# State-space mixer: the second half's outputs in other PSUM tiles, products within a chunk first, the chunk table's products in one run

## The chip, the cores and the metric

The kernel runs on one core of a Trainium2 chip. The metric is the time of one execution on the device, in microseconds (us). The core's engines run side by side, each through its own queue in order: TensorE (PE: matmuls, with weight loads as PEld), VectorE (DVE), ScalarE (ACT), GpSimd (POOL) and SyncE (SP), which here issues nearly all DMAs. Matmuls write to PSUM, whose contents VectorE and ScalarE read.

## What is computed

Two decoder layers over 512 tokens of width 1024. Each runs three token mixers on the same input projection: A (RWKV-7), B (retention) and C, a diagonal complex state-space mixer (S5) in 32 groups of 16 channels and 64 states. Only C is touched:

```python
bu_re = jnp.einsum('gpc,bsgc->bsgp', bb_re, uf)
bu_im = jnp.einsum('gpc,bsgc->bsgp', bb_im, uf)
...
_, _, x_re, x_im = lax.associative_scan(combine, (a_re, a_im, bu_re, bu_im), axis=1)
y = (jnp.einsum('gcp,bsgp->bsgc', c_re.astype(f32), x_re)
     - jnp.einsum('gcp,bsgp->bsgc', c_im.astype(f32), x_im)
     + d_skip.astype(f32) * uf)
y = jax.nn.gelu(y.reshape(bsz, seq, C_WIDTH))
y = y * jax.nn.sigmoid(y @ w_glu.astype(f32) + b_glu.astype(f32))
```

## The kernel before

Mixer C cuts the 512 tokens into 64 chunks of 8. A scan over chunks gives the state ahead of each chunk; the output of a chunk is then a product with that state (a *lag product*, L490) plus a product with the chunk's own inputs through a table (a *product within a chunk*, L495). The groups are worked in two halves (`hf`) of 8 pairs.

`s5_prep` makes the tables. `ca` (powers times C), in four quarters on VectorE and POOL; `ba` (powers times B), turned by PE transposes (L402) and copied by ScalarE (L403); and the table `tt` (s5tt) for the products within a chunk. For `tt`, PE multiplies `bd` by `ca` for four m, two parts and four column strips (L411, one PSUM tile p); ScalarE copies the result to `s1gs` (L414), VectorE adds the skip term (L416), SP writes it to DRAM as gsc (L419) and reads it back in eight transfers, each into 16 partitions of s5tt (L423).

`s5_main` does for each half: 64 input products on PE (L460: `bre` in a PSUM tile m, `bim` in a tile p, 32 in each half of the groups); on VectorE four products that read them (L464 to L467), two scans (L471, L472) and the states `cx` (L479 to L484, after POOL's memsets of their first columns); then on PE into two PSUM tiles b the lag products (L490, 32 in the code, 64 instructions) and the products within a chunk (L495, 16 in the code, 32 instructions). Each of the two results goes through a GELU of two ScalarE and three VectorE steps (L500 to L504), and out to DRAM (yst, L506). Behind both halves four tiles yg are read back (L512) and split by ScalarE and VectorE (L179, L180 in `split`), and `s5_glu` multiplies them.

PSUM has four kinds of tiles, g, m, p and b, two of each. `cx` and the GELU's tile cg exist once, so their next use waits for the last one's end.

Around mixer C, PE works through blocks of the input projection (`proj_steps`): each loads a weight block (raw, L148), splits it (wh by ScalarE at L151, wl by VectorE at L155) and runs 24 matmuls (L169 to L171) into a tile g, which ScalarE evacuates (L609 and L610 for mixer A, L1078 for the gates). A scheduler with its own timeline of the program sets each engine's order from priorities when the program is built; on the chip each engine then keeps to that order and waits on semaphores. The blocks around `s5_main` are called g_1538, g_1572, g_1606 and g_1640 in layer 0 and g_10521 to g_10623 in layer 1, after their PSUM tiles. With two tiles g, g_1640 takes the room of g_1572 and can start when that is evacuated.

Of the kernel before, what the change touches and what calls it, by code (L numbers as in the profile page):

```python
# [80 lines left out]
class Hybrid:  # L81
# [224 lines left out]
    def s5_prep(self, pool, keep):  # L306
# [3 lines left out]
        nc, par = self.nc, self.par  # L310
        V, G, S, PE = nc.vector, nc.gpsimd, nc.scalar, nc.tensor
# [93 lines left out]
        gs = t("gs", (128, 4, 256))  # L405
        G.memset(gs[:, :, 0:128], 0.0)
        ps = self.pps().rearrange("p (m x) -> p m x", m=4)
        for m in range(4):
            for part in range(2):
                for j in range(4):  # L410
                    PE.matmul(ps[32 * j:32 * j + 32, m, :], lhsT=bd[part][:, 4 * m + j].rearrange("p g c -> p (g c)"),  # L411
                              rhs=self.ca[part][:, 4 * m + j, 0:8, :].rearrange("p k c -> p (k c)"), start=part == 0,
                              stop=part == 1, tile_position=(0, 32 * j))
        S.copy(out=gs[:, :, 128:256], in_=ps)  # L414
        for m in range(4):
            V.scalar_tensor_tensor(gs[:, m, 128:144], self.K[:, K_E16:K_E16 + 16], par[:, P_CD + m:P_CD + m + 1],  # L416
# [28 lines left out]
    def s5_main(self, pool, keep):  # L445
        nc, par = self.nc, self.par
        V, G, S, PE = nc.vector, nc.gpsimd, nc.scalar, nc.tensor
        page = lambda tag, bufs=1, dt=F32: pool.tile([128, T], dt, tag=tag, bufs=bufs, name=self.nm(tag))
        n8 = lambda t: t.rearrange("p (r n) -> p r n", n=64)
        H = (slice(0, 64), slice(64, 128))  # L450
        yst = self.dram.tile([4, 128, T], F32, name=self.nm("yst"))
        out = yst.rearrange("m (r g c) (t n) -> t c g (m r) n", g=2, c=16, t=8)
        for hf in range(2):
            prs = slice(8 * hf, 8 * hf + 8)
            bre, bim = self.mps(), self.pps()
            for part, b in ((0, bre), (1, bim)):
                for i in range(8):
                    for g in range(2):
                        pr = 8 * hf + i
                        PE.matmul(b[H[g], 64 * i:64 * i + 64], lhsT=self.ba[:, part, pr, 64 * g:64 * g + 64],  # L460
                                  rhs=self.uc[:, 2 * pr + g, :], start=True, stop=True)
            c, s, dec = (x[:, prs].rearrange("p r n -> p (r n)") for x in (self.rc, self.rs, self.dec))
            t1, t2, t3, t4 = page("c1"), page("c2"), page("c3"), page("c4")
            V.tensor_tensor(t1, bre, c, op=MUL)  # L464
            V.tensor_tensor(t4, bre, s, op=MUL)
            V.tensor_tensor(t2, bim, s, op=MUL)
            V.tensor_tensor(t3, bim, c, op=MUL)  # L467
            V.tensor_tensor(t1, t1, t2, op=ADD)
            V.tensor_tensor(t3, t3, t4, op=SUB)
            zr, zi = page("c2"), page("c4")  # L470
            V.tensor_tensor_scan(zr, dec, t1, 0.0, op0=MUL, op1=ADD)  # L471
            V.tensor_tensor_scan(zi, dec, t3, 0.0, op0=MUL, op1=ADD)  # L472

            x = [page("cx%d" % i).rearrange("p (r n) -> p r n", n=64) for i in range(2)]
            t5, t6 = page("c1"), page("c3")
            for v in x:
                G.memset(v[:, :, 0:1], 0.0)
            d = lambda v: n8(v)[:, :, 0:63]
            V.tensor_tensor(x[0][:, :, 1:], d(zr), d(c), op=MUL)  # L479
            V.tensor_tensor(d(t5), d(zi), d(s), op=MUL)  # L480
            V.tensor_tensor(x[1][:, :, 1:], d(zr), d(s), op=MUL)
            V.tensor_tensor(d(t6), d(zi), d(c), op=MUL)
            V.tensor_tensor(x[0][:, :, 1:], x[0][:, :, 1:], d(t5), op=SUB)
            V.tensor_tensor(x[1][:, :, 1:], x[1][:, :, 1:], d(t6), op=ADD)  # L484
            yp = [self.bps(), self.bps()]
            for i in range(8):
                for part in range(2):
                    for g in range(2):
                        ca = self.ca[part][H[g], 8 * hf + i, 1:9, :].rearrange("p k c -> p (k c)")
                        PE.matmul(yp[g][:, 64 * i:64 * i + 64], lhsT=ca, rhs=x[part][H[g], i, :],  # L490
                                  start=i == 0 and part == 0, stop=False, skip_group_check=True)
            for g in range(2):
                for i in range(8):
                    gr = 2 * (8 * hf + i) + g
                    PE.matmul(yp[g][:, 64 * i:64 * i + 64], lhsT=self.tt[:, gr, :], rhs=self.uc[:, gr, :],  # L495
                              start=False, stop=True, skip_group_check=True)
            for g in range(2):

                ps, y, g1 = yp[g], page("cy", 2), page("cg1")
                S.activation(g1, ps, AF.Square)  # L500
                V.tensor_scalar(g1, g1, 0.044715, 1.0, op0=MUL, op1=ADD)
                V.tensor_tensor(g1, g1, ps, op=MUL)
                S.activation(g1, g1, AF.Tanh, scale=math.sqrt(2.0 / math.pi))
                V.scalar_tensor_tensor(y, g1, 1.0, ps, op0=ADD, op1=MUL)  # L504
                for t in range(8):
                    nc.sync.dma_start(out=out[t, :, g, prs], in_=n8(y)[16 * t:16 * t + 16])  # L506
        self.yg = []
        yhl = keep.tile([128, 2, 4, T], F32R, tag="s5ba", name=self.nm("cyhl"))
        yh, yl = ([yhl[:, i, m, :] for m in range(4)] for i in range(2))
        for m in range(4):  # L510
            y = page("cyg", 4)
            nc.sync.dma_start(out=y, in_=yst[m])  # L512
            self.split(yh[m], yl[m], y, 0.5)
            self.yg.append(y)
        self.yghl = yh, yl
# [823 lines left out]
```

## Time and profile before

| | |
|---|---|
| time, median of 3 runs | 2138.72 us (2137.79 to 2141.57) |
| the profiled execution, its time | 2140.92 us |
| its span, first to last instruction | 2138.8 us |
| mean granted TensorE clock | 0.983 of full speed |
| PE busy | 2081.7 us, 97% |
| VectorE / ScalarE / POOL busy | 57% / 35% / 7% |
| PE's wait for L504 ahead of L490 | 4.6 us in 4 waits |

The page counts busy time on each engine. The lists of waits say which instruction an engine waited for, the timeline lists instructions in order of time, and the rows by stretches give busy time, the granted TensorE clock (1.00 is 2.4 GHz, 0.50 is 1.2 GHz) and what the DMA engines moved. Mixer C's main part lies at 116 to 168 us in layer 0 and at 1178 to 1231 us in layer 1. A wait of an engine that is not on the path to the end costs nothing; here PE is on it nearly all the time.

### The profile page before, as it was taken

The numbers are of one execution on the slowest core, as the hardware profiler recorded it, in microseconds if no ns is written. First come the engines' busy times: TensorE is split into PE (matmuls) and PEld (weight loads), VectorE is DVE, ScalarE is ACT, GpSimd is POOL, SyncE is SP. The second block draws the span as 40 slices with busy tenths as digits, with TensorE's granted clock in tenths as the row PEclk, the third lists the DMA queues.
The fourth block names the chain that finished last, engine by engine and source line by source line (L and its number), as shares of the span: only waits on it lengthen the run. The fifth ranks groups of instructions, "written<-read, shape, count | busy, mean of one in ns | idle before, by whom it ended". The sixth has DMA issues, their size and how long they took to land.

```text
span 2138.8 us, 31693 instructions
## 1 busy us (share of the span) xinstructions
PE 2081.7 (97%) x12784; PEld 1717.1 (80%) x12784; DVE 1220.4 (57%) x2048; ACT 744.0 (35%) x1079; POOL 145.3 (7%) x302
## 2 busy tenths in 40 slices
PE   8999999999999999999999999999999999999998
PEld 7788887787787888888887887787787878888886
DVE  7764467675656734343596534676756666343345
ACT  4423344343332323133254234433333324132231
POOL 1300022021000000000013000220220000000000
PEclk9999999999999999999999899999999999999999
DMA  9584642233655323223274856332335453233331
GB/s 220 149 139 144 192 120 73 88 86 80 197 155 196 100 88 118 73 97 110 96 183 132 120 174 177 99 95 74 93 108 185 148 168 119 80 108 89 99 114 53
DMA packets 365170, 263.95 MB, mean 123 GB/s; under 512 B 79328, under 2 KB 309856, under 8 KB 364896
## 3 DMA queue, kind: packets, MB, share of 16 engines
q1 hardware_dynamic: 365024, 261.93, 43.7%
q8 instruction: 100, 1.64, 0.3%
q14 instruction: 46, 0.38, 0.1%
HBM read 218.89 MB, written 42.99 MB: 122 GB/s over the span
## 4 chain that ended last, share of the span: by engine, by line
PE 85%; DVE 8%; DMA 3%; issue 2%; ACT 2%; SPq 0%; DVEq 0%; ACTq 0%
PE g L169 24%; PE g L170 24%; PE g L171 23%; DVE wl L155 2%; PE b L1038 1%; PE m L731 1%; PE p L899 1%; PE b L1018 1%; ACT wh L151 1%; PE p L883 1%; PE p L872 1%; PE b L171 1%; PE b L170 1%; DMA raw<-in_w_out 1%; PE b L169 1%
## 5 line engine op out<-in xcount | busy, mean ns | idle before, releaser
L151 ACT CAST wh<-raw 128x1024 fp32r<-128x1024 f32 x312 | 326.4, 1051 | 788.3 <-PE g L170 387.4
L169 PE MATMUL g<-xh,wh 128*128 128x512 f32 (+1 forms) x1472 | 579.2, 394 | 8.2 <-DVE bg L1000 3.3
L155 DVE TENSOR_TENSOR wl<-raw,wh 128x1024 fp32r<-128x1024 f32 x312 | 382.9, 1232 | 345.5 <-ACT wh L151 339.2
L170 PE MATMUL g<-xl,wh 128*128 128x512 f32 (+1 forms) x1472 | 566.3, 385 | 0.2
L171 PE MATMUL g<-xh,wl 128*128 128x512 f32 (+1 forms) x1472 | 565.4, 384 | 0.0
L169 PEld LDWEIGHTS g<-xh,wh 128*128 128x128 f32 x1472 | 279.4, 190 | 69.2 <-issue 7.0
L171 PEld LDWEIGHTS g<-xh,wl 128*128 128x128 f32 x1472 | 279.4, 190 | 55.5 <-issue 1.2
L170 PEld LDWEIGHTS g<-xl,wh 128*128 128x128 f32 x1472 | 280.0, 190 | 54.2 <-issue 3.5
L170 PE MATMUL g<-wl,hh 128*128 128x512 f32 x512 | 201.2, 394 | 1.4 <-DVE wl L155 1.4
L171 PE MATMUL g<-wh,hl 128*128 128x512 f32 x512 | 201.1, 393 | 0.0
L169 PE MATMUL g<-wh,hh 128*128 128x512 f32 x512 | 200.2, 392 | 0.0
L170 PEld LDWEIGHTS g<-wl,hh 128*128 128x128 f32 x512 | 96.3, 188 | 24.3 <-DVE wl L155 2.2
L169 PEld LDWEIGHTS g<-wh,hh 128*128 128x128 f32 x512 | 96.2, 188 | 22.0
L171 PEld LDWEIGHTS g<-wh,hl 128*128 128x128 f32 x512 | 96.1, 188 | 21.3
L169 PE MATMUL g<-yh,wh 128*128 128x512 f32 x256 | 104.1, 407 | 0.0
L1281 DVE TENSOR_TENSOR yb<-yb,g 128x512 f32<-128x512 f32 x48 | 32.9, 686 | 121.9 <-PE g L171 121.9
L171 PE MATMUL g<-yh,wl 128*128 128x512 f32 x256 | 100.0, 391 | 0.0
L170 PE MATMUL g<-yl,wh 128*128 128x512 f32 x256 | 99.8, 390 | 0.0
L791 POOL TENSOR_TENSOR TLt<-NL,TL 128x120 f32<-128x120 f32 (+14 forms) x120 | 49.1, 409 | 643.5 <-DMA NL<-nsc 634.7
L169 PE MATMUL g<-wh,xh 128*128 128x256 f32 x256 | 77.1, 301 | 0.4 <-DVE bsw L971 0.3
L170 PE MATMUL g<-wl,xh 128*128 128x256 f32 x256 | 72.4, 283 | 0.0
L171 PE MATMUL g<-wh,xl 128*128 128x256 f32 x256 | 72.2, 282 | 0.0
(346 smaller groups left out, 2746.6 us busy)
## 6 DMA issues: line engine op xcount, KB each, us to landing
raw<-in_w_in SPq DMA_DIRECT2D x132, 512.0 KB, 4.1
raw<-in_w_ff SPq DMA_DIRECT2D x128, 512.0 KB, 4.1
raw<-in_w_branch SPq DMA_DIRECT2D x32, 512.0 KB, 4.3
gs<-gth SPq DMA_DIRECT2D x48, 256.0 KB, 2.3
gth<-gs SPq DMA_DIRECT2D x48, 256.0 KB, 3.1
raw<-in_w_out SPq DMA_DIRECT2D x16, 512.0 KB, 5.4
zs<-az SPq DMA_DIRECT2D x24, 256.0 KB, 4.2
s5tt<-gsc SPq DMA_DIRECT2D x16, 256.0 KB, 12.0
```

The lines of the kernel that those rows point to most:

```text
L151: nc.scalar.copy(out=wh, in_=raw)
L155: eng.tensor_tensor(wl, raw, wh.bitcast(F32), op=SUB)
L169: mm(out, lhsT=wh, rhs=xh, start=first, stop=False)
L170: mm(out, lhsT=wh, rhs=xl, start=False, stop=False)
L171: mm(out, lhsT=wl, rhs=xh, start=False, stop=last)
L731: PE.matmul(ps[h][:, i, :].rearrange("p (s i) -> p s i", i=64), lhsT=BK[H[h], c, :], rhs=rhs, start=True, stop=True)
L791: G.tensor_tensor(tmp[:, :, 0:n], NL[:, s:s + 1, s + 1:16].to_broadcast([128, 8, n]), TL[:, :, s:s + 1].to_broadcast([128, 8, n]), op=MUL)
L872: PE.matmul(ps[H[h], i, :].rearrange("p (s i) -> p s i", i=64), lhsT=Pt[H[h], 4 * g + i, :], rhs=AVX[H[h], h:3:2 - h, 4 * g + i, :], start ...
L883: PE.matmul(ps[H[h], i, :], lhsT=WM[H[h], 4 * g + i, :], rhs=AB[H[h], h, 4 * g + i, :], start=True, stop=True)
L899: PE.matmul(ps[:, h, :], lhsT=AB[:, h, c, :], rhs=AVX[:, h, c, :], start=h == 0, stop=c == 0, skip_group_check=True)
L1018: PE.matmul(ps[:, 0:n], lhsT=k[:, 128 * jc:128 * jc + 128], rhs=q[:, 128 * jc:T], start=True, stop=True)
L1281: V.tensor_tensor(y[t][:, s], y[t][:, s], ps, op=ADD)
```

## The change

The second half's two outputs are put into a tile m and a tile p, whose earlier contents are the first half's inputs `bre` and `bim`; the first half keeps tiles b. The products within a chunk are written ahead of the lag products and open the accumulation. In `s5_prep` the products for the table are chained in one order by `after` (an order on PE without a semaphore), the m with the last quarter of `ca` first.

```diff
--- before.py
+++ after.py
@@ -405,12 +405,18 @@
         gs = t("gs", (128, 4, 256))
         G.memset(gs[:, :, 0:128], 0.0)
         ps = self.pps().rearrange("p (m x) -> p m x", m=4)
-        for m in range(4):
+
+        last = None
+        for m in (3, 0, 1, 2):
             for part in range(2):
                 for j in range(4):
                     PE.matmul(ps[32 * j:32 * j + 32, m, :], lhsT=bd[part][:, 4 * m + j].rearrange("p g c -> p (g c)"),
                               rhs=self.ca[part][:, 4 * m + j, 0:8, :].rearrange("p k c -> p (k c)"), start=part == 0,
                               stop=part == 1, tile_position=(0, 32 * j))
+                    ins = nc.cur_bb.bb.instructions[-1]
+                    if last is not None:
+                        self.after(ins, last)
+                    last = ins
         S.copy(out=gs[:, :, 128:256], in_=ps)
         for m in range(4):
             V.scalar_tensor_tensor(gs[:, m, 128:144], self.K[:, K_E16:K_E16 + 16], par[:, P_CD + m:P_CD + m + 1],
@@ -482,18 +488,19 @@
             V.tensor_tensor(d(t6), d(zi), d(c), op=MUL)
             V.tensor_tensor(x[0][:, :, 1:], x[0][:, :, 1:], d(t5), op=SUB)
             V.tensor_tensor(x[1][:, :, 1:], x[1][:, :, 1:], d(t6), op=ADD)
-            yp = [self.bps(), self.bps()]
+
+            yp = [self.bps(), self.bps()] if hf == 0 else [self.mps(), self.pps()]
+            for g in range(2):
+                for i in range(8):
+                    gr = 2 * (8 * hf + i) + g
+                    PE.matmul(yp[g][:, 64 * i:64 * i + 64], lhsT=self.tt[:, gr, :], rhs=self.uc[:, gr, :],
+                              start=i == 0, stop=False, skip_group_check=True)
             for i in range(8):
                 for part in range(2):
                     for g in range(2):
                         ca = self.ca[part][H[g], 8 * hf + i, 1:9, :].rearrange("p k c -> p (k c)")
                         PE.matmul(yp[g][:, 64 * i:64 * i + 64], lhsT=ca, rhs=x[part][H[g], i, :],
-                                  start=i == 0 and part == 0, stop=False, skip_group_check=True)
-            for g in range(2):
-                for i in range(8):
-                    gr = 2 * (8 * hf + i) + g
-                    PE.matmul(yp[g][:, 64 * i:64 * i + 64], lhsT=self.tt[:, gr, :], rhs=self.uc[:, gr, :],
-                              start=False, stop=True, skip_group_check=True)
+                                  start=False, stop=part == 1, skip_group_check=True)
             for g in range(2):
 
                 ps, y, g1 = yp[g], page("cy", 2), page("cg1")
```

The chunk table's products on PE in layer 0, before: L411 is the group of four matmuls of one m and one part, p_638 its PSUM tile, g_1085 and g_1122 are projection blocks of mixer A, m_600 and m_619 (L402) transposes for `ba`. The last of the eight groups, early in g_1122; the one before it stands eight matmuls ahead:

```order
L171 MATMUL g_1085<-xh_84,wl_1083 128x512
L169 MATMUL g_1122<-xh_84,wh_1118 128x512
L411 MATMUL p_638<-s5ca_73_514,s1bd_71_506 32x128 x4
L170 MATMUL g_1122<-xl_85,wh_1118 128x512
L171 MATMUL g_1122<-xh_84,wl_1120 128x512
```

The same place of the change (L413 is L411's new line), in block g_1159, the next one:

```order
L413 MATMUL p_638<-s5ca_73_514,s1bd_71_506 32x128 x4
L413 MATMUL p_638<-s5ca_72_513,s1bd_70_505 32x128 x4
L413 MATMUL p_638<-s5ca_73_514,s1bd_71_506 32x128
L402 MATMUL m_619<-ident,s1bp_614 128x128 x4
L413 MATMUL p_638<-s5ca_73_514,s1bd_71_506 32x128 x3
L413 MATMUL p_638<-s5ca_72_513,s1bd_70_505 32x128 x4
L171 MATMUL g_1159<-xh_84,wl_1157 128x512
```

Before, the eight groups lie one by one among the blocks g_900 to g_1122. Now one lies near the end of g_1122, and the other seven (28 matmuls) in one run after the fifth matmul of g_1159, with one group of transposes inside; 19 matmuls of g_1159 and the 24 of g_1196 stand between the run and the input products. In layer 1 the run lies after the 17th matmul of g_10105.

The input products on PE in layer 0 before (m_1232, p_1233 for the first half, m_1372, p_1373 for the second), with what follows; xh and xl are the split input:

```order
L460 MATMUL m_1232<-uc_376,s5ba_515 64x64 x15
L460 MATMUL p_1233<-uc_376,s5ba_515 64x64 x16
L460 MATMUL m_1372<-uc_376,s5ba_515 64x64 x16
L460 MATMUL p_1373<-uc_376,s5ba_515 64x64 x16
L169 MATMUL g_1538<-xh_84,wh_1534 128x512
```

And of the change (L460 is L466 now, L495 is L496, L490 is L502), with what each waits for:

```order
L466 MATMUL m_1372<-uc_376,s5ba_515 64x64 x13
L496 MATMUL b_1292<-uc_376,s5tt_678 128x64 [waits DMAHW5_49,DMAHW4_49,DMAHW6_49,DMAHW3_49,DMAHW7_49,DMAHW2_49,DMAHW1_49]
L496 MATMUL b_1292<-uc_376,s5tt_678 128x64 x7
L496 MATMUL b_1293<-uc_376,s5tt_678 128x64 x8
L466 MATMUL m_1372<-uc_376,s5ba_515 64x64 x2
L466 MATMUL p_1373<-uc_376,s5ba_515 64x64 x16
L496 MATMUL m_1432<-uc_376,s5tt_678 128x64 [waits DVE_49,PE_49]
L496 MATMUL m_1432<-uc_376,s5tt_678 128x64 x7
L496 MATMUL p_1433<-uc_376,s5tt_678 128x64 [waits DVE_49,PE_49]
```

Before, the input products are followed by blocks g_1538 and g_1572 (48 matmuls), the first half's L490 and L495, 19 matmuls of g_1606, the second half's L490 and L495, and the last five of g_1606. Now the first half's products within a chunk stand inside the input products, behind the DMAs of s5tt, and the second half's right behind them; then come 15 matmuls of g_1538, the first half's lag products, 9 and 11 of g_1538 and g_1572, the second half's lag products, 13 of g_1572, the 24 of g_1606, and g_1640. In layer 1 L496 stands behind all 32 input products of the first half and ahead of the second half's.

ScalarE in layer 0 before: L500 and L503 are the GELU's square and tanh, L179 the splits of yg, L151 and L1078 the cast and the evacuation for the blocks:

```order
L151 CAST wh_1670<-raw_1668 128x1024
L1078 ACTIVATE gth_1597<-g_1572,hbg_1529 128x512
L500 ACTIVATE cg_222_1343<-b_1292 128x512
L503 ACTIVATE cg_222_1343<-cg_222_1343 128x512
L500 ACTIVATE cg_224_1358<-b_1293 128x512
L503 ACTIVATE cg_224_1358<-cg_224_1358 128x512
L179 ACTIVATE cyhl_1512<-cyg_1513 128x512
L179 ACTIVATE cyhl_1512<-cyg_1517 128x512
```

And of the change (L507 and L510 are the square and the tanh now, L1085 the evacuation):

```order
L151 CAST wh_1636<-raw_1634 128x1024
L1085 ACTIVATE gth_1563<-g_1538,hbg_1529 128x512
L507 ACTIVATE cg_224_1358<-b_1293 128x512
L510 ACTIVATE cg_224_1358<-cg_224_1358 128x512
L507 ACTIVATE cg_240_1483<-m_1432 128x512
L179 ACTIVATE cyhl_1512<-cyg_1513 128x512
L179 ACTIVATE cyhl_1512<-cyg_1517 128x512
L510 ACTIVATE cg_240_1483<-cg_240_1483 128x512
L507 ACTIVATE cg_242_1498<-p_1433 128x512
L510 ACTIVATE cg_242_1498<-cg_242_1498 128x512
L151 CAST wh_1670<-raw_1668 128x1024
L1085 ACTIVATE gth_1597<-g_1572,hbg_1529 128x512
```

The cast wh_1670 and the evacuation of g_1572 have moved from ahead of the GELUs to behind the two splits and the second half's first GELU. In layer 1 these two stand ahead of the last tanh instead of behind it.

On VectorE the second half's last state products still stand ahead of the first half's GELU. On SP, gsc and the eight reads of s5tt move behind one more weight block and one more store of mixer A; one store of a gate and one weight block stand among the stores of yst.

## Rows read from the trace of the kernel before

**Rows 1.** The page, busy time, share of the span and instructions.
```profile
PE 2081.7 (97%) x12784; PEld 1717.1 (80%) x12784; DVE 1220.4 (57%) x2048; ACT 744.0 (35%) x1079; POOL 145.3 (7%) x302
```

**Rows 2.** Waits of PE: total us, times, longest us.
```profile
PE b L490 <- DVE cy L504: 4.6, 4, 2.3
```

**Rows 3.** Timeline of PE, layer 0, second half: start us, us, what [idle before].
```profile
152.57 6.49 PE L490 MATMUL b<-cx,s5ca 64*128 64x64 f32 x54 [2.03 <-DVE cy L504]
158.99 7.09 PE L495 MATMUL b<-uc,s5tt 128*128 128x64 f32 x32
165.84 0.77 PE L170 MATMUL g<-xl,wh 128*128 128x512 f32 x1
...
168.12 0.63 PE L169 MATMUL g<-xh,wh 128*128 128x512 f32 x1
```

**Rows 4.** Timeline of PE, layer 0, first half.
```profile
137.16 3.79 PE L490 MATMUL b<-cx,s5ca 64*128 64x64 f32 x64
140.87 3.79 PE L495 MATMUL b<-uc,s5tt 128*128 128x64 f32 x32
```

**Rows 5.** PE by stretches: us, busy us (count), granted clock, DMA share, GB/s.
```profile
152.50:159.00 6.50, 6.43 (x55) 0.55 0.34 56
...
165.80:170.20 4.40, 4.40 (x12) 0.50 0.28 47
170.20:175.00 4.80, 4.80 (x22) 0.99 0.79 217
```

**Rows 6.** Timeline of PE, layer 1, the first matmul of g_10623.
```profile
1230.80 0.63 PE L169 MATMUL g<-xh,wh 128*128 128x512 f32 x1
```

**Rows 7.** Timeline of PE, layer 0, around one group of L411.
```profile
101.31 0.40 PE L170 MATMUL g<-xl,wh 128*128 128x512 f32 x1
...
102.34 0.40 PE L169 MATMUL g<-xh,wh 128*128 128x512 f32 x1
```

**Rows 8.** Input products: PE by the stretch (layer 0), their first timeline row (layer 1).
```profile
122.17:126.05 3.88, 3.88 (x128) 1.00 1.23 185
...
1184.31 1.09 PE L460 MATMUL m<-uc,s5ba 128*64 128x64 f32 x29
```

**Rows 9.** Timeline of ScalarE, the copies of the table, layers 0 and 1.
```profile
105.81 0.58 ACT L414 COPY s1gs<-p 128x512 f32<-128x512 f32 x1
...
1167.94 0.58 ACT L414 COPY s1gs<-p 128x512 f32<-128x512 f32 x1
```

**Rows 10.** SP's issues of s5tt; the last one's KB and us to landing, each layer.
```profile
112.30 1.38 SPq L423 DMA_DIRECT2D s5tt<-gsc  x3
...
122.35 1.50 SPq L423 DMA_DIRECT2D s5tt<-gsc  x1
s5tt<-gsc SPq DMA_DIRECT2D x1, 256.0 KB, 16.2
...
1185.42 1.21 SPq L423 DMA_DIRECT2D s5tt<-gsc  x1
s5tt<-gsc SPq DMA_DIRECT2D x1, 256.0 KB, 14.9
```

**Rows 11.** All engines by stretches; the last three numbers: clock, DMA share, GB/s.
```profile
108.00:110.00 2.00, 2.00 (x10) 1.66 (x9) 0.62 (x1) 0.00 (x0) 0.00 (x0) 1.00 0.96 299
126.00:138.60 12.60, 12.60 (x77) 10.38 (x74) 12.60 (x20) 2.27 (x3) 0.00 (x0) 1.00 1.26 107
```

**Rows 12.** Timelines of VectorE and ScalarE, layer 0, GELUs and splits.
```profile
143.88 0.67 DVE L479 TENSOR_TENSOR cx<-c,s5rc 128x504 f32<-128x504 f32 x1
...
151.74 0.69 DVE L504 SCALAR_TENSOR_TENSOR cy<-cg,b 128x512 f32<-128x512 f32 x1 [0.69 <-ACT cg L503]
...
161.91 1.22 ACT L179 ACTIVATE cyhl<-cyg 128x512 fp32r<-128x512 f32 x2 [10.21 <-DMA cyg<-yst]
165.03 0.63 ACT L503 ACTIVATE cg<-cg 128x512 f32<-128x512 f32 x1 [1.42 <-DVE cg L502]
...
168.88 0.63 ACT L503 ACTIVATE cg<-cg 128x512 f32<-128x512 f32 x1
```

## The prediction

> **What bounds the kernel now.** The page first: TensorE (PE) is busy 97% of the span [rows 1], so what PE loses, the kernel loses. Then the list of what PE waited for. The wait that the change can remove is there: the second half's lag products (L490) wait for VectorE's last GELU step of the first half (L504), 4.6 us in four waits [rows 2]. PE's timeline shows more than the wait. In layer 0 PE idles 2.03 us, then 54 of the 64 lag products take 6.49 us and the 32 products within a chunk (L495) 7.09 [rows 3]; in the first half 64 and 32 take 3.79 us each [rows 4]. The stretches say why: from 152.5 to 170.2 us the granted clock is 0.50 to 0.55, the 1.2 GHz level, and it is back at 2.4 GHz only after a run of ordinary matmuls [rows 5]. Against the first half's rate that is 2.0 idle, 3.3 and 3.3 in the products and 1.9 in the matmuls behind: 10.5 us per layer could be won. Below I follow one start in each layer: the first matmul of a projection block (g_1640 in layer 0, g_10623 in layer 1), from which on PE has the same work in the same order before and after. It is at 168.12 and 1230.80 us [rows 3, 6].
>
> **Part 1, the chunk table's products (L411) in one run.** Before, eight groups of eight instructions per layer stand between ordinary matmuls, which step by 0.227 us (4.80 us hold 22 records [rows 5]). From the L170 ahead of a group to the second matmul behind it are 1.03 us [rows 7] where two steps would be 0.45: a group costs 0.57, of which I count 0.2 for the two changes of shape and 0.36 as its own, 0.045 per instruction. After, one early group (0.57) and a run of 56 (2.5 + 0.2) cost 3.3 us instead of 4.6; a transpose group moves into the run and a lone input product joins its fellows, 0.4 more. PE comes 1.7 us earlier to the input products in layer 0, 1.2 in layer 1. But the run begins with the pairs whose data come last, so all of it stands late. In layer 0, 43 ordinary matmuls and a transpose group (10.4 us) stand between its end and the input products, which now start at 122.17 - 1.7 = 120.5 [rows 8]: it ends at 110.1. ScalarE copied the table at 105.81 [rows 9]; now at 110.2, **4.4 us later**. In layer 1, 55 matmuls, a transpose group and a lone product (13.4 us) before 1184.31 - 1.2 = 1183.1 [rows 8] give 1169.7, and a copy 1.9 later than at 1167.94 [rows 9].
>
> **Part 2, products within a chunk first.** They read the table s5tt, which goes through DRAM and comes back in eight transfers (L423): first issue 112.30, last issue 122.35, which lands 16.2 us later, at 138.55; in layer 1 1185.42 + 14.9 = 1200.3 [rows 10]. Before, two projection blocks and the lag products hide this: L495 starts at 140.87 [rows 4]. After, L496 stands behind 46 of the 64 input products and ahead of both blocks. PE is there at 120.5 + 92/126 of 3.88 us [rows 8] = 123.3. The table lands 4.4 us later than before, less 1 because an activation store no longer stands among the transfers: 142. In layer 1 PE is there at 1183.1 + 1.9 = 1185.0, the table at 1200.3 + 1.9 = 1202.2. **PE waits 18.7 and 17.2 us**, and everything queued behind L496 on PE waits with it, 48 ordinary matmuls among it. The cover is gone, and the 1.7 us of part 1 only lengthen the wait.
>
> Could the table come much sooner? While little else moves, the DMA engines carry 107 GB/s; eight transfers of 256 KB are 2.1 MB, 20 us by that. In a stretch of weight loads they carry 299 [rows 11], 7 us by that. I keep the measured landing, since the transfers are the same. The Trainium skill (DMA: Bandwidth & Descriptors, Specifications) gives line rate from 512 B up and 435 GB/s as the fabric's ceiling; by that the table would take 4.8 us, an estimate, and the wait would nearly vanish. This trace does not agree: 107 GB/s. The skill's table for partitions 0 to 15 (SBUF — State Buffer, its measured bandwidths by partitions) has 104 GB/s, and each of these transfers fills 16 partitions.
>
> **Part 3, restart.** After an idle 2.03 us PE resumed at half clock, and neither L490 nor L495 brought it back in 13 us [rows 3, 5]; after 18 us I take the same. So half rate for L496 (6.85 us from 158.99 to 165.84 [rows 3]), for the input products left (36 instructions, 2.2 us; in layer 1 64, 3.9), for the second half's L496 (6.85), then ordinary matmuls, 4.4 us of them slow [rows 5], the rest at 0.227: 5.4 us for 15, 5.6 for 16. The first half's lag products follow at full rate, 3.75 [rows 4]. They end at **E = 142 + 25.1 = 167.1**, in layer 1 at 1202.2 + 26.9 = 1229.1.
>
> **Part 4, the new PSUM rooms.** The wait for L504 goes: the second half's outputs need only what VectorE has read long before. What is late next is ScalarE. The evacuation of block g_1572, whose room g_1640 needs, and a weight cast now stand behind the two splits of yg (L179), and these wait for GELU results to go to DRAM and back; before, both stood ahead. After E, VectorE does the second half's last state products and the two GELUs: 143.88 to 152.43 before, 8.5 us [rows 12], plus 0.4 for POOL's memset ahead and 0.9 for ScalarE's cast and evacuation between: E + 9.8. From L504's end to L179 it was 152.43 to 161.91, 9.5 us [rows 12], and SP has two more DMAs among the stores (0.8): E + 20. Two splits 1.2, a tanh, tanh to tanh 3.85 [rows 12], cast and evacuation 1.7: about **E + 26**; in layer 1, where the cast stands two steps earlier, E + 24. PE is there after 20 matmuls, the second half's lag products and 37 (36) matmuls: E + 17.3 (17.0). So it waits another 8.7 and 7.0 us.
>
> **The sum.** Layer 0: 167.1 + 26 = 193.1 against 168.1, +25.0; matmuls at half clock behind the second wait lose 2.1 against 1.0 before, +1.1. Layer 1: 1229.1 + 24 = 1253.1 against 1230.8, +22.3, and +1.6. Together **+50 us**. The profiled execution took 2140.9 us, 2.2 more than the median of the runs, with the span of 2138.8 in the table above; the differences are within the span, so the changed kernel's own profile would read 2191, and I add them to the median: 2138.7 + 50 = 2188.7, say **2188**. Bounds: the landing by 2 us either way is 4 us in two layers; a clock that comes back during L496 saves up to 5 us per layer.
>
> **Rivals.** (a) *Only the first wait.* If ScalarE's chain is through by E + 17, PE restarts late and does not stop again: layer 0 184.4 - 168.1 - 1.0 = +15.3, layer 1 +14.9; **2169**. For it: many of the chain's steps can overlap. Against: its trip through DRAM alone is 9.5 us. Partial waits lie between.
> (b) *The table is there in time: faster.* 2.1 MB would have to come in the 6.6 us between a first issue at 116.7 and PE's arrival, at 320 GB/s, three times what these transfers get [rows 11]. Then E is 139.1 and 1201.9, old wait and slow stretch are gone, and ScalarE's chain sets the blocks: 165.1 and 1226.0, -3.0 and -4.8, with +2.7 for slow restarts: **2133.6**; without the second waits too, 2114. It decides at a landing before about 125 us; beyond, the half-clock restart eats the gain. The skill's line rate (DMA: Bandwidth & Descriptors) would lead here; the row of 107 GB/s speaks against it.
> (c) *More stops.* The second pair of splits could hold up evacuations too; 3 us per stop and layer, and the time is over **2199**.
> (d) *No visible change.* The gain and a short wait would have to cancel, with a landing near 125; nothing shows that.
>
> **How the numbers follow.** Forecast 0.61, (a) with partial waits 0.25, (c) 0.07, (b) 0.05, (d) 0.02. The range takes in the forecast with its bounds and most of (a): 2163 to 2199. About 0.2% (4 us) is what a measurement can tell from no change: faster 0.05, same 0.02, slower 0.93.
>
> **What would show it.** Right: on PE one wait of 15 to 20 us per layer ahead of L496, ended by the DMA of s5tt; granted clock 0.50 for some 20 us behind it; no wait for L504; a second wait ahead of g_1640, ended by ScalarE's L1085; the first transfer of s5tt issued at about 116.7. Wrong: if L496 starts within 5 us of the input products, part 2 falls; full clock in L496 takes 9 us per layer off E; L1085 ahead of PE leaves (a).

## The result: 33 us slower, and the profile after

The changed kernel takes 2173.59 us (median of 4 runs, 2171.04 to 2175.60), the kernel before 2140.14 beside it (2137.79 to 2142.26): a ratio of 1.0165, 95% interval 1.0153 to 1.0178. Forecast were 2188 us and a range of 2163 to 2199. The sign, the two stops and layer 0 came as worked out; the time forecast was 14 us too high, and most of that lies in layer 1. One of the four runs of e3 below took 2587.34 us at a mean granted clock of 0.746, and it is left out of e3's row.

The page of the changed kernel, which answers to [rows 1], shows a longer span with the same work on PE: it is busy 3 us less and idle 38 us more.

```profile
span 2173.8 us, 31683 instructions
PE 2078.3 (96%) x12784; PEld 1718.9 (79%) x12784; DVE 1220.0 (56%) x2048; ACT 743.2 (34%) x1079; POOL 151.6 (7%) x302
```

What PE waited for in the changed kernel (us in total, times, longest); in place of the 4.6 us for L504 in [rows 2] stand a wait for the table and one for ScalarE's evacuation:

```profile
PE b L496 <- DMA s5tt<-gsc: 29.9, 2, 18.6
PE g L169 <- ACT gth L1085: 14.3, 2, 8.7
```

PE's timeline in the changed kernel (start, us, line, operation, in brackets the idle time and what ended it): layer 0 first, then, from 1207.58 on, layer 1. Ordinary matmuls (those of the projection blocks, 128x512), the other input products and the second half's lag products are left out.

```profile
121.29 1.15 PE L466 MATMUL m<-uc,s5ba 128*64 128x64 f32 x32
...
142.79 7.06 PE L496 MATMUL b<-uc,s5tt 128*128 128x64 f32 x32 [18.60 <-DMA s5tt<-gsc]
...
151.90 3.68 PE L496 MATMUL m<-uc,s5tt 128*128 128x64 f32 x16
155.37 3.62 PE L496 MATMUL p<-uc,s5tt 128*128 128x64 f32 x16
...
163.29 3.79 PE L502 MATMUL b<-cx,s5ca 64*128 64x64 f32 x64
...
192.89 0.79 PE L169 MATMUL g<-xh,wh 128*128 128x512 f32 x1 [8.72 <-ACT gth L1085]
...
1207.58 1.09 PE L466 MATMUL m<-uc,s5ba 128*64 128x64 f32 x29
...
1220.93 7.06 PE L496 MATMUL b<-uc,s5tt 128*128 128x64 f32 x32 [11.28 <-DMA s5tt<-gsc]
...
1231.54 2.46 PE L496 MATMUL m<-uc,s5tt 128*128 128x64 f32 x16
1233.83 1.95 PE L496 MATMUL p<-uc,s5tt 128*128 128x64 f32 x16
...
1239.43 3.79 PE L502 MATMUL b<-cx,s5ca 64*128 64x64 f32 x64
...
1265.71 0.79 PE L169 MATMUL g<-xh,wh 128*128 128x512 f32 x1 [5.63 <-ACT gth L1085]
```

The first half's L496 takes 7.06 us in both layers, half rate. The second half's takes 7.1 us in layer 0, but 4.2 in layer 1: there the clock came back in its middle. The rows by stretches say the same (PEclk is the number ahead of the last two):

```profile
142.80:159.20 16.40, 16.40 (x101) 16.16 (x102) 7.15 (x11) 0.00 (x0) 0.00 (x0) 0.50 0.06 13
159.20:163.20 4.00, 4.00 (x15) 2.97 (x14) 1.26 (x2) 0.00 (x0) 0.00 (x0) 0.81 0.02 4
...
1221.00:1230.00 9.00, 9.00 (x70) 8.88 (x72) 0.00 (x0) 0.00 (x0) 0.00 (x0) 0.50 0.22 53
...
1232.00:1234.00 2.00, 2.00 (x18) 2.00 (x17) 2.00 (x4) 0.00 (x0) 0.00 (x0) 0.87 0.04 8
```

ScalarE and SP around the two stops in layer 0. ScalarE is idle for 9.62 us ahead of the splits (L179), which wait for yg from DRAM, and the evacuation that g_1640 needs (L1085 at 192.16) stands behind them:

```profile
110.96 0.59 ACT L420 COPY s1gs<-p 128x512 f32<-128x512 f32 x1 [0.66 <-PE p L413]
...
186.11 1.29 ACT L179 ACTIVATE cyhl<-cyg 128x512 fp32r<-128x512 f32 x2 [9.62 <-DMA cyg<-yst]
...
192.16 0.68 ACT L1085 ACTIVATE gth<-g,hbg 128x512 f32<-128x512 f32 x1
```

```profile
112.34 0.36 SPq L425 DMA_DIRECT2D gsc<-s1gs  x1
116.80 4.23 SPq L429 DMA_DIRECT2D s5tt<-gsc  x6
```

**Where the 35 us lie.** Setting the starts of PE's matmuls of equal rank in the two traces side by side gives the delay along the program: +24.8 us at g_1640 and +26.4 after its slow restart; +24.3 in the middle of the kernel; +34.9 at g_10623, +36.6 after the restart, +35.0 at the end. So layer 0 costs 26.4 (forecast 26.1), layer 1 costs 12.3 (forecast 23.9), and 2.1 and 1.6 us come back in between and behind. Some of that is the clock too: the half-clock stretch that lies at 327 us before lasts 6.8 us, its counterpart after, at 355 us, 3.4. The other way round, a half-clock stretch of 3.4 us at 1099 us, ahead of mixer C's part, has no counterpart before; just behind it the delay is 25.5, so about 1.2 of layer 1's 12.3 us is not the change's doing.

### The profile page after: what moved, and what is told of

The parts are those of the page before. It is cut to its first block, busy times and chain, and to the rows that moved or that the text cites. A ratio compares the mean times of both kernels' runs of the same rounds, so it can differ in the third digit from the quotient of the medians.

```text
span 2173.8 us, 31683 instructions
## 1 busy us (share of the span) xinstructions
PE 2078.3 (96%) x12784; PEld 1718.9 (79%) x12784; DVE 1220.0 (56%) x2048; ACT 743.2 (34%) x1079; POOL 151.6 (7%) x302
## 4 chain that ended last, share of the span: by engine, by line
PE 85%; DVE 6%; DMA 4%; ACT 2%; issue 2%; SPq 1%; DVEq 0%; ACTq 0%
PE g L169 24%; PE g L170 23%; PE g L171 23%; DVE wl L155 2%; PE b L1045 1%; DMA s5tt<-gsc 1%; PE m L738 1%; PE p L906 1%; ACT wh L151 1%; PE b L1025 1%; PE p L879 1%; PE p L890 1%; PE b L171 1%; PE b L170 1%; SPq L429 1%
## 5 line engine op out<-in xcount | busy, mean ns | idle before, releaser
L151 ACT CAST wh<-raw 128x1024 fp32r<-128x1024 f32 x312 | 326.3, 1051 | 744.8 <-PE g L170 356.7
L170 PEld LDWEIGHTS g<-wl,hh 128*128 128x128 f32 x512 | 96.3, 188 | 24.3 <-DVE wl L155 2.3
```

The lines of the kernel that those rows point to most:

```text
L151: nc.scalar.copy(out=wh, in_=raw)
L170: mm(out, lhsT=wh, rhs=xl, start=False, stop=False)
```

## The experiments

Theory: PE stops for the table's landing, because L496 stands ahead of what covers it, runs at half clock behind that, and stops again for an evacuation that stands behind ScalarE's splits. Rivals: the new PSUM tiles or the new order of work on PE cost the time by themselves; the run of the table's products costs it; the small products (those of 64 columns: input, lag and within a chunk) bring the clock down by themselves. Times are medians; ratios are to the kernel before on the same chip, with 95% intervals.

| kernel | us | ratio |
|---|---|---|
| e1 new tiles alone | 2143.06 | 1.0022 (1.0011 to 1.0033) |
| e2 products within a chunk first, alone | 2162.91 | 1.0129 (1.0105 to 1.0153) |
| e3 tiles and order | 2164.43 | 1.0134 (1.0109 to 1.0158) |
| e4 the table's products in one run, alone | 2131.13 | 0.9971 (0.9960 to 0.9982) |
| the change, all three | 2173.59 | 1.0165 (1.0153 to 1.0178) |
| e5 table read in spread-out transfers | 2185.48 | 1.0232 (1.0206 to 1.0258) |
| e6 PE kept at work in layer 0 | 2170.30 | 1.0153 (1.0133 to 1.0174) |
| e7 evacuation ahead of the splits | 2163.52 | 1.0125 (1.0110 to 1.0140) |
| e12 all three, PE's order by hand | 2127.07 | 0.9951 (0.9935 to 0.9968) |
| e9 the same, ScalarE's order too | 2114.76 | 0.9901 (0.9875 to 0.9926) |
| e8 tiles, lag products first, orders by hand | 2122.73 | 0.9929 (0.9914 to 0.9944) |
| e10 e8 with the run | 2117.94 | 0.9899 (0.9881 to 0.9916) |

### One part at a time (e1 to e4)

e1, the new tiles alone:

```diff
-            yp = [self.bps(), self.bps()]
+            yp = [self.bps(), self.bps()] if hf == 0 else [self.mps(), self.pps()]
```

> Only the PSUM tiles of the second half's outputs are changed; the products within a chunk stay behind the lag products and the chunk table's products where they were. The scheduler now puts the second half's lag products right behind the first half's products within a chunk, ahead of the 19 matmuls that stood between. Theory (two waits: the table's landing and ScalarE's splits, each with a stretch at half clock behind it): the table is covered as before, so no wait for it; PE stands ready at about 144.7 us and the second half's states at 146.6, a wait of about 1.9 us in place of 2.0 for the GELU. If that short wait again costs the clock, the time stays at about 2140; if not, PE wins up to 8 us per layer, 2124. Rival (the new tiles themselves, or the order of PE that they allow, cost the time): over 2150.

The wait for L504 is gone, and another has taken its place: the lag products of the second half, now free to go early, go so early that they wait for their states (PE's timeline of e1).

```profile
147.02 0.29 PE L490 MATMUL m<-cx,s5ca 64*128 64x64 f32 x1 [0.77 <-DVE cx L483]
...
148.33 0.44 PE L490 MATMUL m<-cx,s5ca 64*128 64x64 f32 x1 [0.87 <-DVE cx L484]
```

Behind these 1.6 us the clock is down again: 0.53 on average from 147.0 to 165.2. So nothing is won there, and waits of 2.1 and 5.0 us for an evacuation come on top, more than the 6 us by which e1 is slower (0.2%). Alone the tiles do no good; that they do no harm by themselves is argued from these waits, and e8 bears it out.

e2, the order within a half alone: the loop of the products within a chunk written ahead of the lag products, all in tiles b.

> Only the order within a half is changed: products within a chunk ahead of the lag products, both halves in tiles b, the table's products as before. Theory: the first half's products within a chunk stand behind the first half's input products and wait for the table: landing 138.6 less PE's arrival at about 124.5 is 14 us in layer 0, about 13 in layer 1, then half clock for up to 10 us of work; the second half keeps its wait for the GELU. 2165 to 2180. Rival (the table is not the cause): about 2140, no wait for s5tt.

The wait for the table is there without the other two parts, 14.2 us in layer 0 and 12.9 in layer 1 (waits of e2; 14 and 13 expected). The second half's wait for the GELU, which was to stay, is gone, and e2 lies just under the 2165 expected:

```profile
PE b L489 <- DMA s5tt<-gsc: 27.2, 2, 14.2
```

e3, tiles and order, without the run:

> The change without the one run of the table's products (that loop stays as in the kernel before). Theory: table waits of about 14 and 13 us instead of 18.6 and 11.3, second wait behind the two splits about 9 and 6 us, 2165 to 2175. If the one run were the cause of the loss: about 2140 or below.

Waits of 13.8 and 13.2 us for the table, of 6.8 and 6.1 for the evacuation. This is most of the loss (1.3% of 1.65%), so the run is not its main cause; what the run adds to e3, 0.3%, is within the intervals.

e4, the run alone: the diff's first piece and nothing else.

> Only the one run of the table's products. Theory: the table lands at 142 instead of 138.6 in layer 0 while PE comes 1.7 us earlier to the products within a chunk (139.2): a wait of about 3 us there and perhaps half clock behind, none in layer 1; 2137 to 2147. If the run alone were what costs: over 2150.

Faster than expected. The late table did cost a stop, of 2.81 us (PE's timeline of e4). The profile names no releaser, but the last transfer, issued at 127.42, took 13.3 us to its landing (SP's issues of e4), that is until 140.72:

```profile
134.21 3.79 PE L495 MATMUL b<-cx,s5ca 64*128 64x64 f32 x64
...
140.81 6.35 PE L500 MATMUL b<-uc,s5tt 128*128 128x64 f32 x32 [2.81 <-issue]
```

```profile
s5tt<-gsc SPq DMA_DIRECT2D x1, 256.0 KB, 13.3
```

```profile
144.00:151.80 7.80, 7.80 (x27) 6.74 (x27) 3.61 (x6) 2.30 (x4) 0.00 (x0) 0.50 0.36 77
151.80:162.00 10.20, 10.20 (x107) 9.46 (x106) 1.43 (x3) 1.74 (x3) 0.00 (x0) 1.00 0.32 79
```

But behind it stand only the 32 products within a chunk and then ordinary matmuls, the clock is back at 151.8, and PE comes to the second half's lag products late enough not to wait for L504. In layer 0 one stop of 2.8 us with 10 us of half clock took the place of one of 2.0 with 17. In layer 1 there is no wait for the table, and the wait for the GELU stays, 2.25 us, with 13.7 us of half clock where it was 17.1. The run itself helps too: counted from just ahead of it, PE comes to the input products 2.1 us earlier in layer 0 and 2.2 in layer 1.

### The first wait and the clock (e5, e6, e11)

e5, the same bytes read back in sixteen transfers, each into 8 partitions spread over all 128; PE's order nearly as in the change, written out. Of its edit, the transfers:

```diff
-        for b in range(8):
-            nc.sync.dma_start(out=self.tt[16 * b:16 * b + 16], in_=rows[:, :, 16 + 16 * b:144 + 16 * b])
+        for c in range(16):
+            r0 = rows[c, :, 16:144]
+            src = bass.AP(tensor=r0.tensor, offset=r0.offset, ap=[[16, 8]] + [list(x) for x in r0.ap])
+            nc.sync.dma_start(out=self.tt.rearrange("(b c) g x -> c b g x", c=16)[c], in_=src)
```

> The changed kernel with its order on PE around the two halves written out, and the table read back in sixteen transfers that each fill 8 partitions spread over all 128, in place of eight that each fill 16 partitions in a row; bytes and rows of 512 B are the same. Theory: the transfer into 16 neighbouring partitions is what holds the table at about 107 GB/s, and the table's landing sets the first wait: the transfers run at 200 GB/s or more, the table lands at about 128 us in layer 0 and the wait falls from 18.6 to under 5 us, 2135 to 2155. Rival (the read from DRAM in rows of 512 B sets the rate): landing at about 142 and a wait of 18 us again, 2170 to 2176. If the wait falls and the time does not, the first wait was not on the path.

The table came later, not sooner: waits of 24.4 and 18.7 us (first row, PE's timeline). From 116 to 150 us, with two weight blocks among the transfers, the DMA engines moved 93 GB/s, and the time of their packets adds up to 60.1% of 16 engines' (the rows of the changed kernel, 116 to 146 us, stand below: 106 GB/s and 107.6%; the packets' times are added up, so the sum can pass 100%).

```profile
147.56 1.73 PE L468 MATMUL b<-uc,s5tt 128*128 128x64 f32 x7 [24.37 <-DMA s5tt<-gsc]
```

```profile
DMA packets 6305, 3.16 MB, mean 93 GB/s; under 512 B 160, under 2 KB 6304, under 8 KB 6304
...
q1 hardware_dynamic: 6304, 3.15, 60.1%
```

```profile
DMA packets 6315, 3.17 MB, mean 106 GB/s; under 512 B 161, under 2 KB 6314, under 8 KB 6314
...
q1 hardware_dynamic: 6314, 3.16, 107.6%
```

So the experiment changed two things. Fewer packets were under way at a time, 9.6 against 17.2 on average (0.601 and 1.076 of 16), and each took less, 52 ns against 82 (9.6 over 34 us shared by 6304 packets, 17.2 over 30 us by 6314). The Trainium skill (DMA: Bandwidth & Descriptors, Why a DMA increments its semaphore by 16 and not by 1) says that the number of engines is the largest up to 16 that divides the outer dimension on both sides, which by that is 8 for these transfers; about half as many packets under way agree with it. That 16 neighbouring partitions hold a packet up is borne out by the 82 ns against 52, but a read by all engines into spread partitions wasn't tried, so what it would bring stays open. The packets' size is hardly the limit: from 134 to 136 us of the changed kernel, with a weight block under way too, 215 GB/s were moved in packets that were all under 2 KB as well. What is shown is that the landing sets the first wait: L496's start in layer 0 moved from 142.79 to 147.56 with it.

e6, 86 ordinary matmuls more ahead of layer 0's first L496, so that PE works through the wait; the rest of PE's order is nearly the change's, written out:

> The changed kernel with the same order on PE written out, and in layer 0 alone 86 matmuls of 128x512 more (19.5 us at 0.227) ahead of the first products within a chunk, into a tile that these then open anew: PE works through the wait for the table. Theory: the half clock behind the first wait comes from PE's idleness; with PE at work the 32 + 32 products within a chunk take 3.8 us each, the 18 input products 1.1 and the 15 matmuls 3.4, so the first half's lag products end at about 159 instead of 167.1, 8 us earlier, and the kernel takes about 2166. Rival (the small products themselves bring the clock down, or the table's transfer does): 0.50 there again and about 2174.

By the medians 3 us are gained, not 8, and the intervals of e6 and the change overlap. The clock stayed full while the table was read (1.00 from 124 to 143), so the transfer does not bring it down. Then came a stop of 0.86 us: L496 (L466 here) began at full clock, which fell to half 2.5 us behind the stop, for 13.7 us (timeline and stretches of e6). That the short stop did this is argued, from e8 and e9 below, where the same products without a stop ran at 1.00.

```profile
144.35 4.79 PE L466 MATMUL b<-uc,s5tt 128*128 128x64 f32 x32 [0.86 <-issue]
```

```profile
124.00:143.00 19.00, 19.00 (x85) 15.70 (x84) 9.38 (x15) 0.63 (x1) 0.00 (x0) 1.00 1.26 123
...
144.35:146.90 2.55, 2.54 (x23) 2.55 (x23) 0.00 (x0) 0.00 (x0) 0.00 (x0) 0.99 0.03 6
146.90:149.20 2.30, 2.30 (x13) 2.18 (x14) 0.00 (x0) 0.00 (x0) 0.00 (x0) 0.50 0.04 7
```

e11, the changed kernel once more, for a second profile:

> The changed kernel again, as it is, for a second profile. Open is why the clock came back 17.9 us after the first wait's end in layer 0 and 11.6 us in layer 1. If the program sets it: 18 and 12 us again. If it varies between executions: in layer 0 anything from 9 to 18, and the span 1 to 5 us off with it. The waits should be 18.6 and 11.3 within 1 us.

Its one run took 2166.63 us, 9.0 us less in span than the first profile. Waits 17.5 and 13.0, further from 18.6 and 11.3 than the 1 us expected; and in layer 0 the clock is back 9.0 us after the restart, where it took 17.9 (end of the half-clock stretch at 160.7) in the first profile, and in layer 1 11.6 both times:

```profile
140.00:149.00 9.00, 8.96 (x68) 8.88 (x68) 0.00 (x0) 0.00 (x0) 0.00 (x0) 0.50 0.11 26
149.00:152.50 3.50, 3.50 (x35) 3.43 (x33) 3.29 (x6) 0.00 (x0) 0.00 (x0) 1.00 0.00 0
```

Over all profiles with a wait of 10 us or more ahead of the products within a chunk (the change twice, e2, e3, e5, e6, e7: thirteen waits), the clock came back 9.0 to 11.6 us after the restart eleven times, amid the small products (in e2 just behind them), and 17.9 and 18.5 us twice. With the same program it differs from execution to execution, so a single profile cannot tell it; what sets it stays open. The Trainium skill (TensorE: Matmul & The Clock Gate, Part 1) says that the number of slow matmuls at a kernel's start varies between runs of one kernel. Here it is a restart in mid-kernel, and the 17.9 and 9.0 us vary likewise.

### The second wait, and the way out (e7 to e10, e12)

e7, the splits held behind the evacuation of the second gate block, as an order on ScalarE without a semaphore:

```diff
+            held.append(nc.cur_bb.bb.instructions[-2])
...
+            if lo == 0 and i == 1:
+                self.evac = nc.cur_bb.bb.instructions[-1]
...
+                        for x in held:
+                            self.after(x, self.evac)
```

> The changed kernel with ScalarE's splits of yg held behind its evacuation of the second gate block (g_1572, g_10555); nothing else is moved by hand. Theory: the second wait is that evacuation standing behind the splits, which wait for a trip through DRAM; held back, PE's waits of 8.7 and 5.6 us ahead of g_1640 and g_10623 go, with the slow restart of 1.6 behind each: 2174 - 17 = 2157, and the first waits stay at 18.6 and 11.3. Rival (another step of ScalarE is as late): under 5 us gained, over 2169.

10 us gained of the 17 expected. PE's wait ahead of g_1640 fell from 8.7 to 0.84 us, and the 5.6 us ahead of g_10623 went, which shows the cause; 3.70 and 2.58 us came back a block later, for the next evacuation, which still stands behind splits (PE's timeline of e7, layer 0), and the first waits, 19.9 and 12.1, were 2 us longer together.

```profile
183.10 0.50 PE L169 MATMUL g<-xh,wh 128*128 128x512 f32 x1 [0.84 <-ACT gth L1087]
198.00 0.50 PE L169 MATMUL g<-xh,wh 128*128 128x512 f32 x1 [3.70 <-ACT gth L1087]
```

e8, tiles of the change, lag products first, and PE's order chained by hand: `s5_main` takes the steps of the gate blocks and draws 48 matmuls behind the input products and 21 between the halves; the splits stand behind the second GELU.

```diff
+        for _ in range(16):
+            next(fill)
...
+            for _ in range(7 * hf):
+                next(fill)
+            yp = [self.bps(), self.bps()] if hf == 0 else [self.mps(), self.pps()]
```

> The new tiles of the second half, lag products first and the chunk table's products as in the kernel before, and PE's order written out: input products, 48 ordinary matmuls, the first half's products, 21 ordinary matmuls, the second half's products; ScalarE's splits stand behind the second half's GELU. Theory: no wait ahead of either half's products (states at 146.6 us, PE there at about 149.5), so no half clock from 153 to 170: 10.5 us less per layer, 2117; with a late evacuation in between 2125. Rival (the products of 64 columns alone bring the clock down): half clock as before, the wait of 2.0 alone gone, 2133.

No half clock in mixer C's part of either layer; both halves' products run at full rate (first two rows, stretches of e8). The 17 us at half clock in [rows 5] are gone, and that without a change in the products, which speaks against the rival that these alone bring the clock down. What keeps it from 2117 are waits of 0.96 us in layer 0 and 3.15 in layer 1 for evacuations behind a split. Behind the 3.15 us stand ordinary matmuls, and the clock stays at 1.00 (last two rows, timeline and stretch).

```profile
149.00:158.00 9.00, 9.00 (x104) 8.38 (x103) 3.26 (x7) 2.46 (x4) 0.00 (x0) 1.00 0.34 56
158.00:165.00 7.00, 7.00 (x33) 5.77 (x32) 5.60 (x8) 5.55 (x8) 0.00 (x0) 1.00 0.58 151
```

```profile
1229.34 0.50 PE L169 MATMUL g<-xh,wh 128*128 128x512 f32 x1 [3.15 <-ACT gth L1094]
```

```profile
1229.00:1240.00 11.00, 10.66 (x47) 8.78 (x48) 3.41 (x3) 3.46 (x5) 0.00 (x0) 1.00 0.70 206
```

e12, all three parts of the change, with 81 ordinary matmuls drawn ahead of the products within a chunk and 24 between the lag products; nothing else:

> All three parts of the change with PE's order alone written out as in e9 (81 ordinary matmuls ahead of the products within a chunk, 24 between the lag products), and ScalarE's order left to the scheduler: two splits now stand ahead of the second half's last GELU. Theory: the first wait and its half clock go by PE's order alone; the later ScalarE order costs at most a wait of some 5 us per layer for an evacuation: 2115 to 2125. Rival (e9 owes its gain to ScalarE's order): 2145 or more.

Faster than the kernel before by 0.5%, a little less than the 2125 expected: the first wait is gone, and the second remains, 4.7 and 7.6 us; one of 2.1 stands ahead of them (waits of e12).

```profile
PE g L169 <- ACT gth L1108: 14.5, 3, 7.6
```

e9 orders ScalarE as well (splits behind the second GELU, the last two behind the fifth gate block's evacuation):

> All three parts of the change, with PE's order written out so that 81 ordinary matmuls (three blocks and a part) stand between the input products and the first products within a chunk, 24 between the two halves' lag products, and ScalarE's splits behind the second half's GELU, the last two behind the evacuation of the fifth gate block. Theory (nothing is wrong with products within a chunk first, but for their standing ahead of what covers the table): no wait for s5tt (PE there at about 141.5 us, the table at 140.8 to 142), no half clock, no second wait; of the changed kernel's 2174 go the waits of 18.6 and 11.3, about 16 at half clock and 17 of second waits and restarts, 2112; since the GELU then comes some 10 us later, the gate of mixer C's output may wait for yg, about 5 us per layer, 2122. Rival (the order itself, or the tiles, cost time): over 2137.

1.0% faster. PE's timeline and stretch of e9 in layer 0: no wait ahead of the products within a chunk, and 1.00 in them. The stop of 3.15 us, for an evacuation that stands behind the cast of a weight block queued among the table's transfers, is followed by ordinary matmuls, and the clock was down for 3.4 us only.

```profile
144.62 0.75 PE L169 MATMUL g<-xh,wh 128*128 128x512 f32 x1 [3.15 <-ACT gth L1112]
...
148.38 3.68 PE L466 MATMUL b<-uc,s5tt 128*128 128x64 f32 x32
151.89 1.95 PE L466 MATMUL m<-uc,s5tt 128*128 128x64 f32 x16
```

```profile
148.40:155.50 7.10, 7.10 (x65) 7.09 (x63) 0.96 (x1) 0.30 (x1) 0.00 (x0) 1.00 0.51 151
```

That PE did not wait for the table in layer 0 is in part luck. The last transfer landed at 145.4 us, where 140.8 to 142 was expected; without that stop and the 1.7 us lost at half clock behind it PE would have been there at about 143.5 (an estimate from these rows: 148.38 - 3.15 - 1.7). In layer 1 the table landed at 1185.0, 8.8 us ahead of its first use. And the second wait is not quite gone: 2.0 us for an evacuation remain in each layer.

e10, e8 with the run, 63 matmuls ahead and 9 between, and the last two splits held too:

> The written-out order of the run before (lag products first, new tiles, splits behind the GELU), with the chunk table's products in one run, 63 ordinary matmuls ahead of the first half's products, 9 between the halves, and the last two splits held behind the fifth gate block's evacuation. Theory: 3.2 and 1.0 us of waits for that evacuation go, the run gives 1.7 and 1.2 us, the table lands within 1 us of PE: 2122.7 - 7 = 2116. If a wait of about 1 us for the table brings the clock down, 5 to 8 us more in that layer, 2123.

As good as e9 within the intervals. A stop of 0.53 us ahead of the first half's products within a chunk did not bring the clock down (PE's timeline and stretch of e10).

```profile
144.75 3.76 PE L508 MATMUL b<-uc,s5tt 128*128 128x64 f32 x32 [0.53 <-issue]
```

```profile
140.00:160.00 20.00, 19.47 (x213) 17.92 (x212) 13.04 (x19) 7.18 (x11) 0.23 (x2) 1.00 0.69 149
```

So either order will do once it is covered: with all parts of the change the kernel can be faster than before, and the place in which the scheduler put them lost the time. A written-out order with the old tiles was not run, so how much of the 1.0% needs the new tiles and how much is the order's alone stays open.

## Why the prediction was right in sign and too high in size

- **Part 1, the run.** Right where it was sized: L466 starts at 121.29 (120.5 forecast); layer 1's, less 24.3, at 1183.3 (1183.1); the copies at 110.96 (110.2) and 1169.7 (1169.7). Two errors meet in these starts: the run gains 2.1 and 2.2 us, counted from just ahead of it, not 1.7 and 1.2, and in both layers a half-clock stretch ahead of it (at 14 and 1099 us), which the profile before lacks, takes more than the difference away again. That the run could by itself speed the kernel up by more than its own gain (e4) I had not seen: it moves a stop to where ordinary matmuls follow sooner.
- **Part 2, the first wait.** Layer 0: 18.60 us against 18.7. Layer 1: 11.28 against 17.2; this term was mis-sized. L496 started at 1220.93 - 24.3 = 1196.6 instead of 1202.2. Of the 5.6 us, 2.2 are an earlier first issue (2.98 us behind gsc's write, where it was 4.95 before) and 3.4 a faster transfer, 22.5 us from first issue to L496's start where 25.9 from first issue to landing were taken over from before. The weight loads moved about among the eight transfers; that this made the difference isn't shown. The bound of 2 us on the landing was too narrow.
- **Part 3, the restart.** Layer 0 hit E exactly: L502 ends at 167.1. Layer 1 did not: from L496's start to E were 22.3 us, not 26.9, as the clock came back amid the second half's L496. I had put that as a bound (up to 5 us per layer); e11 and the other profiles show that it is the commoner case, and that layer 0's hit was luck: in e11 E comes 20.1 us after L496's start there, not 24.3. "I take the same" as after a stop of 2 us was the step that failed; it rested on one program's two stops.
- **Part 4, the second wait.** As argued: the wait for L504 is gone, ScalarE's splits hold up the evacuation, 8.72 and 5.63 us (8.7 and 7.0 forecast); g_1640 at 192.89 (193.1). e7 shows the cause. The hit owes something to a slip: the terms listed add up to about E + 27, not E + 26. The splits came at E + 19.0 instead of E + 20 and the two tanhs 3.4 us apart instead of 3.85, so that the evacuation ended at E + 25.8. The restarts cost 1.6 and 1.7 us (1.1 and 1.6).
- **The sum.** +50 against +35.0 in the spans: layer 1's landing 5.6, its clock 4.6, its second chain 1.5 (E + 22.5, not 24), and 3.7 that came back outside the mixer, less 0.3 in layer 0 and 0.1 in layer 1's restart.
- **The rivals.** (b) needed a landing at 125; it came at 142.7. (a) named nearly the right time, 2169, but by the wrong mechanism: the second waits were there. (c) fell, for no third stop for an evacuation stands in either layer. The line rate of the Trainium skill (DMA: Bandwidth & Descriptors, Specifications), which would have led to (b), isn't reached by the changed kernel's 106 GB/s either.

## What to carry to other kernels

When an operand comes through DRAM, the order of the products that read it decides whether its trip is covered: moving them ahead of their cover cost 1.3% here (e2); with the same products behind 81 ordinary matmuls the changed kernel gained 0.5 to 1.0% (e12, e9). A freed buffer may only move a stop to the next thing that is late, and here stops of 0.9 to 2.8 us ahead of small products were followed by 10 to 17 us at half clock; look for an order with no stop at all, or one in which ordinary matmuls stand right behind the stop (3.15 us of stop in e8 and e9: 0 and 3.4 us at half clock). Look in the same way at the queue that frees the next buffers: a copy that waits for DRAM must not stand ahead of an evacuation.

## What the runs showed of the hardware

The granted clock fell to 0.50 behind short stops ahead of mixer C's small products: 2.03 us (before), 2.81 (e4), 0.86 (e6), two of 0.77 and 0.87 (e1). Behind one of 0.53 (e10) it stayed at 1.00, and with no stop at all ahead of them (e8, e9) they ran at 1.00. After long waits the half clock ended 9 to 18 us behind the restart, by the execution; after stops of 3.15 us with ordinary matmuls behind them it lasted 3.4 us in e9 and did not come in e8. The read-back of the table (2.1 MB in rows of 512 B, with 1 MB of weight blocks among it) ran at 93 GB/s in transfers of 8 spread partitions (packets' time 60.1% of 16 engines') and at 106 in transfers of 16 neighbouring ones (107.6%), while in a stretch of weight loads the same engines carried 299 [rows 11].
